# An encoder trunk on one core: another order of work in the mixer, and the wide products of gate and up ahead of the narrow ones

## The chip, the core and the metric

The kernel runs on one NeuronCore of a Trainium2 chip. The metric is the device time of one execution in microseconds (us), lower is better. Before the change the median of three runs is 956.33 us (955.96 to 956.51).

PE is the matrix engine (TensorE) and PEld its loads of stationary operands, DVE the vector engine, ACT the scalar engine, POOL GpSimd, SP the queue that issues the loads. PSUM has 8 banks, and each result of PE needs one until DVE or ACT has read it.

## What is computed

Two layers, each of three steps, on x of 256 tokens by 1024 columns, all in float32:

```python
def swiglu(x, w_in, w_out):
    h = x @ w_in
    gate, up = h[..., :D_FF], h[..., D_FF:]
    return (jax.nn.silu(gate) * up) @ w_out
...
    for l in range(DEPTH):
        x = layer_norm(ALPHA * x + 0.5 * swiglu(x, ffn1_w_in[l], ffn1_w_out[l]), ln_g[l, 0], ln_b[l, 0])
        mix = hybrid_mixer(x, cos, sin, mask, w_in[l], w_out[l], ...)
        x = layer_norm(ALPHA * x + mix, ln_g[l, 1], ln_b[l, 1])
        x = layer_norm(ALPHA * x + 0.5 * swiglu(x, ffn2_w_in[l], ffn2_w_out[l]), ln_g[l, 2], ln_b[l, 2])
```

D_FF is 2816. The mixer projects x once and splits the columns into two groups of heads. The first is differential attention: four heads with two score matrices each, softmax of both, the second subtracted with a learned weight, products with v, a root-mean-square norm. The second is attention in a window of 128 positions: eight query heads share two key and value heads, and a sink logit joins each softmax ("local" in the kernel's words). Queries and keys of both get rotary positions. Both outputs go side by side through one output projection.

## The kernel before, in words

**Split products.** Every float32 matrix is split into a high part in a reduced float format and a low remainder: ACT casts a weight tile (wh, line 80, 128x1024), DVE subtracts for the remainder (wl, line 81). A product is the sum of high by high, high by low and low by high. Weights come tile by tile through the class `Weights`: SP loads into 5 raw buffers, wh and wl have 9 buffers each, `get(i)` asks for tiles up to i+8. The casts have the lowest priority: the compiler's scheduler puts them into the queues of ACT and DVE wherever it sees nothing more urgent that is ready. Each queue is worked off in order. PE alone keeps the order of the program text.

**FFN.** `ffn` runs four times. `first` does the first four of 22 column tiles of gate and up for 128 tokens at a time. `col(j)` does each of the other 18, so 72 columns in all: for gate, then for up, 8 wide products (line 350: 512 moving columns, high weights by the high and low parts of x for both token tiles) and 8 narrow ones (line 352: 256 moving columns, low weights by the high part of x). Then ACT and DVE add the two halves, take silu, multiply and split again. `step` does the down projection (line 400), `layer_norm` follows for each token tile t.

**Mixer.** The order of PE's work is a text, `ORDER`, worked off token by token, the same for both layers:

- `P nm t c`: c of the four parts of the projection nm for token tile t (dq, dk, dv, sq: 6 products of 512 columns a part, lines 465 to 467; sk: 6 of 256). After the last part DVE turns the rotary positions (lines 481 to 491).
- `X`, `Z`: transposes of x for t=1 at the start and of the new x for t=0 at the end (line 273). Both need a finished layer norm.
- `T nm t`: transposes of queries or keys (line 501), after which ACT and DVE write the high and low parts (lines 503, 504).
- `S d t`, `S s t`: one unit of scores, 12 products of 64 rows (line 509) in two PSUM banks: two heads on the lower 64 partitions, two on the upper. Softmax follows on DVE and ACT (lines 522 to 535, or 551 to 572).
- `A t u`: 4 transposes of differential attention's weights (line 580), copied out by ACT (line 582). `V t`: its 16 products with v (line 594), then squares on ACT, a power on POOL, and y on DVE (lines 600 to 606).
- `W t n`: of local attention; n=0: 8 transposes (line 580), n=1: the other 8, and the 8 products of unit 0 with v (line 624), n=2: the 8 products of unit 1, after which the result is split (lines 634, 635).
- `Y t`: 4 transposes of y (line 273), split by lines 275 and 276. `O t c`: c of the 8 row tiles of the output projection (6 products each, line 688), and layer norm after the eighth. `G`: loads of the layer norm's constants.

In line 509 the three products of a score (high by high, high by low, low by high) stand together: three for the lower half of the partitions, then three for the upper, and so on.

Of the kernel before, what the change touches and what calls it, by code (L numbers as in the profile page):

```python
# [19 lines left out]
P = 128  # L20
SEQ = 256
D = 1024
KT = D // P
# [21 lines left out]


ORDER = """
P dq 0 3; P dk 0 2; P dq 0 1; P dk 0 1; X; P dk 0 1; P dq 1 1; P dv 1 1; P dv 0 1; P dk 1 1; P dv 0 1; P dv 1 1;
P dk 1 1; P dq 1 1; P dk 1 1; P dv 1 1; P dk 1 1; P dq 1 1; P dv 0 1; P dv 1 1; T dk 0; T dq 0; T dk 1; P sk 1
1; P sk 0 1; P dq 1 1; P dv 0 1; S d 0; S d 0; P sk 0 1; T dq 1; P sk 0 1; P sk 1 2; P sq 0 2; P sk 1 1; S d 1;  # L50
S d 1; P sk 0 1; P sq 0 2; A 0 1; A 0 0; T sk 1; P sq 1 2; T sq 0; T sk 0; V 0; A 1 0; S s 0; P sq 1 1; A 1 1; P
sq 1 1; G; V 1; S s 0; Y 0; T sq 1; O 0 3; S s 1; O 0 1; W 0 0; Y 1; S s 1; W 0 1; W 0 2; O 1 1; W 1 0; O 0 2; O
1 1; O 0 2; W 1 1; W 1 2; O 1 4; Z; O 1 2
"""
# [39 lines left out]
def encoder_kernel(  # L94
# [206 lines left out]
    def ffn(l, n, last=False):  # L301
# [39 lines left out]
        def col(j):  # L341
            nonlocal wi

            hs = [ps.tile([P, 2, SEQ], F32, tag="b", name=f"h{'gu'[s]}_{nm}_{j}") for s in range(2)]
            tl = tp.tile([P, 2, SEQ], F32, tag="tl", name=f"tl_{nm}_{j}", bufs=2)
            for s in range(2):
                wh, wl = W.get(wi)
                wi += 1
                for k in range(KT):
                    mm(hs[s], wh[:, k * P : (k + 1) * P], xx[:, k], start=(k == 0), stop=False)  # L350
                for k in range(KT):
                    mm(hs[s][:, 1, :], wl[:, k * P : (k + 1) * P], xx[:, k, 0], start=False, stop=(k == KT - 1))  # L352
                nc.scalar.copy(tl[:, s], hs[s][:, 1, :])  # L353
                dv.tensor_tensor(tl[:, s], hs[s][:, 0, :], tl[:, s], ALU.add)  # L354
# [77 lines left out]
    def mixer(l):  # L432
# [72 lines left out]

        def qk(o, q, k, a, h, kh, qt):
            b = slice(qt * P, (qt + 1) * P)
            for i, (m, n) in enumerate(((0, 0), (0, 1), (1, 0))):
                mm(o, q[m][a, h, b], k[n][a, kh, :], start=(i == 0), stop=(i == 2))


        def diff_scores(qt, u):
            nm = f"{l}{qt}{u}"
            with tc.high_priority():
                sc = [ps.tile([P, 2, SEQ], F32, tag="b", name=f"sd{nm}{c}") for c in range(2)]
                for i in range(2):
                    for c in range(2):
                        a = slice(64 * c, 64 * c + 64)
                        qk(sc[c][:, i, :], qT, kT, a, 2 * u + i, 2 * u + i, qt)
                mx = sp.tile([P, 4], F32, tag="mx", name=f"mxd{nm}")  # L520
# [17 lines left out]
        def swa_scores(qt, u):  # L538
            nm = f"{l}{qt}{u}"
            with tc.high_priority():  # L540
                sc = [ps.tile([P, 2, SEQ], F32, tag="b", name=f"ss{nm}{v}") for v in range(2)]
                for i in range(2):
                    for v in range(2):
                        a = slice(64 * v, 64 * v + 64)
                        qk(sc[v][:, i, :], sqT, skT, a, 2 * u + i, 0, qt)
                mx = sp.tile([P, 4], F32, tag="mx", name=f"mxs{nm}")
                sk = snk.rearrange("p (v u i) -> p u v i", v=2, u=2)[:, u]
                for v in range(2):
                    for i in range(2):
                        q = 2 * v + i  # L550
                        dv.tensor_tensor_reduce(sc[v][:, i, :], sc[v][:, i, :], mask[:, (1 - qt) * P : (3 - qt) * P], 1.0, sk[:, v, i : i + 1],
                                                ALU.add, ALU.max, mx[:, q : q + 1])
# [7 lines left out]
                den = sp.tile([P, 4], F32, tag="den", name=f"ds{nm}", bufs=8)  # L560
                for v in range(2):
                    for i in range(2):
                        q = 2 * v + i
# [4 lines left out]
                dv.reciprocal(rc, rc)  # L568
                for v in range(2):
                    for i in range(2):  # L570
                        q = 2 * v + i
# [36 lines left out]
        def swa_pv(qt, units):  # L608
# [16 lines left out]

            def part(n):
                with tc.high_priority():
                    if n < 2:
                        tr_(n)
                    if n > 0:  # L630
                        mm_(n - 1)
                    if n == 2:
                        dh = xx[:, 4:8, 0, qt, :]
# [40 lines left out]

        def do_w(q, n):
            if n == 0:
                sw[q] = swa_pv(q, units["s", q])
            sw[q](n)

# [16 lines left out]
        for tok in ORDER.split(";"):  # L696
# [15 lines left out]
            elif op == "V":  # L712
                ok = num("A", ar[0], 0) and num("A", ar[0], 1) and full("dv", 0) and full("dv", 1)
            elif op == "W":
                ok = (ar[1] < 2 or all(full(nm, ar[0]) for nm in heads)) and num("S", "s", ar[0]) > min(ar[1], 1) and (ar[1] == 0 or num("W", ar[0], ar[1] - 1))
            elif op == "Y":
                ok = all(full(nm, ar[0]) for nm in heads) and num("V", ar[0])
            elif op == "O":
                ok = num("Y", ar[0]) and num("G") and (rows(ar[0]) + ar[1] <= 4 or num("W", ar[0], 2))
            elif op == "Z":  # L720
                ok = rows(0) == KT
            else:
                ok = True
# [16 lines left out]
            elif op == "V":  # L740
                diff_pv(ar[0], units["d", ar[0]], pTs[ar[0]], y[ar[0]])
            elif op == "W":
                do_w(*ar)
            elif op == "Y":
# [83 lines left out]
```

## Time and profile before

| | |
|---|---|
| median of three runs | 956.33 us (955.96 to 956.51) |
| the profiled execution, its own time | 955.75 us |
| its span, first to last instruction | 954.0 us |
| PE busy | 942.0 us (99%) |
| DVE busy | 669.2 us (70%) |
| ACT busy | 510.4 us (54%) |
| granted clock of TensorE, mean | 0.998 of full speed |
| chain that ended last, PE's share | 90% |
| first mixer | from about 189.3 us to 290.5 us |
| second mixer | from about 660.3 us to 761.4 us |

A timeline row gives the start of a group of like instructions, its length up to the end of the last one, the engine, the line, the operation, the tiles, the form and the count; in brackets stands the idle time of the engine before it and what ended it. PE's instructions overlap: a wide product is shown as 0.39 us long, while the next one starts some 0.23 us after it. So the pace of PE is read from one start to the next, and not from lengths.

### The profile page before, as it was taken

The numbers are of one execution on the slowest core, as the hardware profiler recorded it, in microseconds if no ns is written. First come the engines' busy times: TensorE is split into PE (matmuls) and PEld (weight loads), VectorE is DVE, ScalarE is ACT, GpSimd is POOL, SyncE is SP. The second block draws the span as 40 slices with busy tenths as digits, with TensorE's granted clock in tenths as the row PEclk, the third lists the DMA queues.
The fourth block names the chain that finished last, engine by engine and source line by source line (L and its number), as shares of the span: only waits on it lengthen the run. The fifth ranks groups of instructions, "written<-read, shape, count | busy, mean of one in ns | idle before, by whom it ended". The sixth has DMA issues, their size and how long they took to land.

```text
span 954.0 us, 13703 instructions
## 1 busy us (share of the span) xinstructions
PE 942.0 (99%) x5087; PEld 801.7 (84%) x5087; DVE 669.2 (70%) x1103; ACT 510.4 (54%) x889; POOL 17.0 (2%) x27
## 2 busy tenths in 40 slices
PE   9999999999999999999999999999999999999997
PEld 6888888888778888888888888888887888888886
DVE  7887754688987776754687767447889877767434
ACT  5767543436765655553356565433477656565420
POOL 0000000000000000000000000000000000000000
PEclk9999999999999999999999999999999999999999
DMA  9886555366316755555376555553743366565521
GB/s 326 311 281 204 195 177 198 124 226 189 106 67 208 260 194 183 193 179 197 126 257 223 189 185 190 183 194 123 260 124 112 114 226 223 188 189 187 179 64 45
DMA packets 51234, 176.42 MB, mean 185 GB/s; under 512 B 6240, under 2 KB 8032, under 8 KB 51168
## 3 DMA queue, kind: packets, MB, share of 16 engines
q1 hardware_dynamic: 50896, 175.42, 56.0%
q8 instruction: 40, 0.66, 0.3%
q14 instruction: 26, 0.21, 0.1%
q10 hardware_dynamic: 272, 0.13, 0.0%
HBM read 174.48 MB, written 1.05 MB: 184 GB/s over the span
## 4 chain that ended last, share of the span: by engine, by line
PE 90%; DVE 6%; ACT 2%; issue 1%; POOL 0%; DVEq 0%
PE acc L400 25%; PE hg L350 14%; PE hu L350 14%; PE hb L318 9%; PE hu L352 7%; PE hg L352 7%; PE ao L688 4%; DVE wl L81 1%; ACT ed L528 1%; PE os L624 1%; PE pj_dq L467 1%; PE pj_dq L466 1%; PE pj_dk L467 1%; PE pj_dq L465 1%; PE pj_dk L466 1%
## 5 line engine op out<-in xcount | busy, mean ns | idle before, releaser
L81 DVE TENSOR_TENSOR wl<-raw,wh 128x1024 fp32r<-128x1024 f32 (+1 forms) x319 | 385.4, 1212 | 210.2 <-ACT wh L80 206.2
L80 ACT CAST wh<-raw 128x1024 fp32r<-128x1024 f32 (+1 forms) x319 | 332.5, 1046 | 323.8 <-PE acc L400 123.7
L400 PE MATMUL acc<-wh,g 128*128 128x512 f32 (+1 forms) x748 | 192.7, 377 | 0.0
L400 PEld LDWEIGHTS acc<-wh,g 128*128 128x128 f32 x748 | 136.0, 188 | 25.8
L350 PE MATMUL hg<-xx,wh 128*128 128x512 f32 x576 | 144.8, 393 | 0.0
L350 PE MATMUL hu<-xx,wh 128*128 128x512 f32 x576 | 144.2, 392 | 0.0
L350 PEld LDWEIGHTS hg<-xx,wh 128*128 128x128 f32 x576 | 103.6, 189 | 18.6
L350 PEld LDWEIGHTS hu<-xx,wh 128*128 128x128 f32 x576 | 103.6, 189 | 18.5
L400 PE MATMUL acc<-wl,g 128*128 128x512 f32 (+1 forms) x374 | 111.3, 377 | 0.0
L352 PEld LDWEIGHTS hg<-xx,wl 128*128 128x128 f32 x576 | 78.6, 190 | 5.7
L352 PEld LDWEIGHTS hu<-xx,wl 128*128 128x128 f32 x576 | 78.6, 190 | 5.6
L352 PE MATMUL hu<-xx,wl 128*128 128x256 f32 x576 | 80.3, 282 | 0.0
L352 PE MATMUL hg<-xx,wl 128*128 128x256 f32 x576 | 80.3, 282 | 0.0
L400 PEld LDWEIGHTS acc<-wl,g 128*128 128x128 f32 x374 | 68.9, 188 | 13.2
L318 PE MATMUL hb<-wh,xx 128*128 128x512 f32 x256 | 70.2, 391 | 0.0
L318 PEld LDWEIGHTS hb<-wh,xx 128*128 128x128 f32 x256 | 47.9, 188 | 10.5 <-ACT wh L80 0.7
L318 PE MATMUL hb<-wl,xx 128*128 128x512 f32 x128 | 39.5, 390 | 0.0
L688 PE MATMUL ao<-wh,xx 128*128 128x512 f32 x128 | 37.6, 400 | 1.1 <-ACT xx L275 1.1
L359 ACT CAST g<-tl 128x256 fp32r<-128x256 f32 x72 | 28.9, 402 | 8.1 <-DVE tl L357 8.0
L357 DVE TENSOR_TENSOR tl<-tl 128x256 f32<-128x256 f32 x72 | 30.5, 424 | 2.2
L354 DVE TENSOR_TENSOR tl<-hu,tl 128x256 f32<-128x256 f32 x72 | 30.0, 417 | 2.8 <-ACT tl L353 2.8
L360 DVE TENSOR_TENSOR g<-tl,g 128x256 fp32r<-128x256 f32 x72 | 30.1, 419 | 2.0 <-ACT g L359 1.9
(182 smaller groups left out, 940.7 us busy)
## 6 DMA issues: line engine op xcount, KB each, us to landing
raw<-in_f_in_dram SPq DMA_DIRECT2D x144, 512.0 KB, 4.1
raw<-in_f_out_dram SPq DMA_DIRECT2D x88, 512.0 KB, 3.4
raw<-in_m_in_dram SPq DMA_DIRECT2D x36, 512.0 KB, 3.5
raw<-in_f_b_dram SPq DMA_DIRECT2D x29, 512.0 KB, 3.4
raw<-in_m_out_dram SPq DMA_DIRECT2D x8, 512.0 KB, 4.5
raw<-in_m_out_dram SPq DMA_DIRECT2D x16, 256.0 KB, 4.2
lng<-in_ln_g_dram SPq DMA_DIRECT2D x6, 512.0 KB, 5.8
lnb<-in_ln_b_dram SPq DMA_DIRECT2D x6, 512.0 KB, 6.1
```

Of the source, the lines that this page charges most:

```text
L80: nc.scalar.copy(wh[:, s], raw[:, s])
L81: nc.vector.tensor_tensor(wl[:, s], raw[:, s], wh[:, s].bitcast(F32), ALU.subtract)
L318: mm(hb[s], xx[:, k, g, t, :], ww[:, 512 * s : 512 * s + 512], start=(k == 0 and e == 0), stop=(k == KT - 1 and e == 2))
L350: mm(hs[s], wh[:, k * P : (k + 1) * P], xx[:, k], start=(k == 0), stop=False)
L352: mm(hs[s][:, 1, :], wl[:, k * P : (k + 1) * P], xx[:, k, 0], start=False, stop=(k == KT - 1))
L354: dv.tensor_tensor(tl[:, s], hs[s][:, 0, :], tl[:, s], ALU.add)
L357: dv.tensor_tensor(gv, tl[:, 0], gv, ALU.mult)
L359: nc.scalar.copy(gs[q][:, jj, 0, :], gv)
L360: dv.tensor_tensor(gs[q][:, jj, 1, :], gv, gs[q][:, jj, 0, :].bitcast(F32), ALU.subtract)
L400: mm(a, g, ww[:, s], start=(k == 0 and e == 0), stop=(k == JT - 1 and e == 2))
L466: mm(o, xx[:, k, 0, t, :], wl[:, s], start=False, stop=False)
L688: mm(acc[t][h], xx[:, k, g, t, :], ww[:, s], start=(k == 0 and e == 0), stop=(k == KT - 1 and e == 2))
```

## The change

Three edits.

1. In `col` both weight tiles are asked for at once, and the order is: 8 wide products of gate, 8 wide of up, 8 narrow of gate, 8 narrow of up. Every product stays.
2. `qk` takes both halves of the partitions: each of the three products of a score is issued for the lower half and then for the upper. In local attention's softmax the loops over the head in the unit (i) and the half (v) change places.
3. The transposes of local attention are a token of their own, `B t n` (8 transposes, unit n), and `W t n` is its 8 products alone (n=0, 1). `ORDER` is a new text. The counts of all other tokens stay.

```diff
 ORDER = """
-P dq 0 3; P dk 0 2; P dq 0 1; P dk 0 1; X; P dk 0 1; P dq 1 1; P dv 1 1; P dv 0 1; P dk 1 1; P dv 0 1; P dv 1 1;
-P dk 1 1; P dq 1 1; P dk 1 1; P dv 1 1; P dk 1 1; P dq 1 1; P dv 0 1; P dv 1 1; T dk 0; T dq 0; T dk 1; P sk 1
-1; P sk 0 1; P dq 1 1; P dv 0 1; S d 0; S d 0; P sk 0 1; T dq 1; P sk 0 1; P sk 1 2; P sq 0 2; P sk 1 1; S d 1;
-S d 1; P sk 0 1; P sq 0 2; A 0 1; A 0 0; T sk 1; P sq 1 2; T sq 0; T sk 0; V 0; A 1 0; S s 0; P sq 1 1; A 1 1; P
-sq 1 1; G; V 1; S s 0; Y 0; T sq 1; O 0 3; S s 1; O 0 1; W 0 0; Y 1; S s 1; W 0 1; W 0 2; O 1 1; W 1 0; O 0 2; O
-1 1; O 0 2; W 1 1; W 1 2; O 1 4; Z; O 1 2
+P dk 0 1; P dq 0 3; P dk 0 1; X; P dk 0 2; P dq 1 1; P dk 1 1; P dq 0 1; P dv 0 1; P dv 1 1; P dq 1 1; P dv 1 1;
+P dq 1 1; P dk 1 3; P dv 0 1; P dv 1 1; P dq 1 1; P dv 1 1; T dk 0; T dq 0; T dk 1; P sk 1 1; P sk 0 1; P dv 0
+2; S d 0; S d 0; T dq 1; P sk 0 2; P sk 1 3; P sq 0 2; T sk 1; P sk 0 1; S d 1; A 0 0; P sq 0 1; A 0 1; S d 1; T
+sk 0; P sq 0 1; P sq 1 2; G; T sq 0; V 0; S s 0; A 1 0; P sq 1 1; A 1 1; P sq 1 1; Y 0; V 1; S s 0; O 0 1; T sq
+1; O 0 3; S s 1; B 0 0; B 0 1; Y 1; W 0 0; W 0 1; S s 1; O 1 1; O 0 1; O 1 1; O 0 3; B 1 0; B 1 1; O 1 1; W 1 0;
+W 1 1; O 1 1; Z; O 1 4
 """
...
+            ws = [W.get(wi), W.get(wi + 1)]
+            wi += 2
             for s in range(2):
-                wh, wl = W.get(wi)
-                wi += 1
                 for k in range(KT):
-                    mm(hs[s], wh[:, k * P : (k + 1) * P], xx[:, k], start=(k == 0), stop=False)
+                    mm(hs[s], ws[s][0][:, k * P : (k + 1) * P], xx[:, k], start=(k == 0), stop=False)
+            for s in range(2):
                 for k in range(KT):
-                    mm(hs[s][:, 1, :], wl[:, k * P : (k + 1) * P], xx[:, k, 0], start=False, stop=(k == KT - 1))
+                    mm(hs[s][:, 1, :], ws[s][1][:, k * P : (k + 1) * P], xx[:, k, 0], start=False, stop=(k == KT - 1))
...
-        def qk(o, q, k, a, h, kh, qt):
+        def qk(os, q, k, h, kh, qt):
             b = slice(qt * P, (qt + 1) * P)
             for i, (m, n) in enumerate(((0, 0), (0, 1), (1, 0))):
-                mm(o, q[m][a, h, b], k[n][a, kh, :], start=(i == 0), stop=(i == 2))
+                for c, o in enumerate(os):
+                    a = slice(64 * c, 64 * c + 64)
+                    mm(o, q[m][a, h, b], k[n][a, kh, :], start=(i == 0), stop=(i == 2))
...
-            def part(n):
+            def part(op, n):
                 with tc.high_priority():
-                    if n < 2:
+                    if op == "B":
                         tr_(n)
-                    if n > 0:
-                        mm_(n - 1)
-                    if n == 2:
+                    else:
+                        mm_(n)
+                    if op == "W" and n == 1:
                         dh = xx[:, 4:8, 0, qt, :]
                         nc.scalar.copy(dh, o)
```

## Rows read from the trace of the kernel before

**Rows 1.** The page, its first part: busy time, share of the span, instructions.

```profile
PE 942.0 (99%) x5087; PEld 801.7 (84%) x5087; DVE 669.2 (70%) x1103; ACT 510.4 (54%) x889; POOL 17.0 (2%) x27
```

**Rows 2.** The chain that ended last, FFN stretches: start, length, instructions.

```profile
27.30 1.81 PE hg L350 x8
...
36.53 1.84 PE hu L350 x8
39.32 1.84 PE hg L350 x8
...
128.71 57.83 PE acc L400 x255
```

**Rows 3.** Timeline of PE, wide products behind 18 narrow ones, first mixer.

```profile
230.76 0.40 PE L465 MATMUL pj_sq<-wh,xx 128*128 128x512 f32 x1
...
232.14 0.39 PE L465 MATMUL pj_sq<-wh,xx 128*128 128x512 f32 x1
```

**Rows 4.** Timeline of PE, scores of differential attention, first mixer.

```profile
225.72 1.69 PE L509 MATMUL sd<-dkT,dqT 64*128 64x256 f32 x24
227.35 0.39 PE L465 MATMUL pj_sk<-wh,xx 128*128 128x256 f32 x1
...
234.31 1.80 PE L509 MATMUL sd<-dkT,dqT 64*128 64x256 f32 x24
236.04 0.39 PE L465 MATMUL pj_sk<-wh,xx 128*128 128x256 f32 x1
```

**Rows 5.** Timeline of PE around T sq 0 and the first S s 0.

```profile
239.61 1.03 PE L580 MATMUL tpd<-ident,ed 128*128 128x128 f32 x8
...
243.13 0.39 PE L467 MATMUL pj_sq<-wh,xx 128*128 128x512 f32 x1
243.74 0.63 PE L501 MATMUL tq_sq<-ident,r_sq 128*128 128x128 f32 x4 [0.22 <-DVE wt L533]
...
244.32 1.95 PE L594 MATMUL od<-vd,pTd 128*128 128x128 f32 x16
...
246.63 0.38 PE L509 MATMUL ss<-skT,sqT 64*128 64x256 f32 x1
247.84 0.98 PE L509 MATMUL ss<-skT,sqT 64*128 64x256 f32 x11 [0.83 <-DVE skT L504]
```

**Rows 6.** Timeline of PE, later in the first mixer: transposes, and an S s 1.

```profile
254.87 0.66 PE L273 MATMUL tr_y<-ident,y 128*128 128x128 f32 x4
...
256.71 0.72 PE L688 MATMUL ao<-wh,xx 128*128 128x512 f32 x2 [0.52 <-ACT xx L275]
...
261.04 0.98 PE L509 MATMUL ss<-skT,sqT 64*128 64x256 f32 x12
...
265.77 0.66 PE L580 MATMUL tps<-ident,esw 128*128 128x128 f32 x4
266.74 0.66 PE L580 MATMUL tps<-ident,esw 128*128 128x128 f32 x4 [0.30 <-DVE xx L276]
...
278.42 1.03 PE L580 MATMUL tps<-ident,esw 128*128 128x128 f32 x8
```

**Rows 7.** Timeline of DVE, 242 to 253 us.

```profile
242.92 0.68 DVE L489 TENSOR_TENSOR r_sq<-m_sq,m_sq 128x512 f32<-128x512 f32 x1
...
244.64 2.35 DVE L81 TENSOR_TENSOR wl<-raw,wh 128x1024 fp32r<-128x1024 f32 x2
...
251.82 0.60 DVE L606 SCALAR_TENSOR_TENSOR y<-od,f,gsb 128x128 f32<-128x128 f32 x2
```

**Rows 8.** Timeline of ACT: the last exponential of the first S s 1.

```profile
267.93 0.54 ACT L564 ACTIVATE esw<-ss,mxs 128x256 f32<-128x256 f32 x1
```

**Rows 9.** Timelines of DVE and PE: ends of two layer norms, and X.

```profile
195.03 1.41 DVE L296 SCALAR_TENSOR_TENSOR x<-x,rs,lnb 128x512 f32<-128x512 f32 x2
...
198.83 1.03 PE L273 MATMUL tr_m<-ident,x 128*128 128x128 f32 x8
...
283.13 1.41 DVE L296 SCALAR_TENSOR_TENSOR x<-x,rs,lnb 128x512 f32<-128x512 f32 x2
```

More of the change, by code (lines that the diff above doesn't have):

```diff
@@ L516, in diff_scores @@
                 for i in range(2):
-                    for c in range(2):
-                        a = slice(64 * c, 64 * c + 64)
-                        qk(sc[c][:, i, :], qT, kT, a, 2 * u + i, 2 * u + i, qt)
+                    qk([s[:, i, :] for s in sc], qT, kT, 2 * u + i, 2 * u + i, qt)
                 mx = sp.tile([P, 4], F32, tag="mx", name=f"mxd{nm}")
@@ L542, in swa_scores @@
                 for i in range(2):
-                    for v in range(2):
-                        a = slice(64 * v, 64 * v + 64)
-                        qk(sc[v][:, i, :], sqT, skT, a, 2 * u + i, 0, qt)
+                    qk([s[:, i, :] for s in sc], sqT, skT, 2 * u + i, 0, qt)
                 mx = sp.tile([P, 4], F32, tag="mx", name=f"mxs{nm}")
                 sk = snk.rearrange("p (v u i) -> p u v i", v=2, u=2)[:, u]
-                for v in range(2):
-                    for i in range(2):
+                for i in range(2):
+                    for v in range(2):
                         q = 2 * v + i
@@ L560, in swa_scores @@
                 den = sp.tile([P, 4], F32, tag="den", name=f"ds{nm}", bufs=8)
-                for v in range(2):
-                    for i in range(2):
+                for i in range(2):
+                    for v in range(2):
                         q = 2 * v + i
@@ L568, in swa_scores @@
                 dv.reciprocal(rc, rc)
-                for v in range(2):
-                    for i in range(2):
+                for i in range(2):
+                    for v in range(2):
                         q = 2 * v + i
@@ L673, in do_a, with do_w @@
                 pTs.setdefault(q, {})[u] = (trans_p(e[:, 0, 0, :], e[:, 0, 1, :], f"d{l}{q}{u}"))
-        def do_w(q, n):
-            if n == 0:
+        def do_w(op, q, n):
+            if q not in sw:
                 sw[q] = swa_pv(q, units["s", q])
-            sw[q](n)
+            sw[q](op, n)
         def do_o(t, c):
@@ L713, in mixer @@
                 ok = num("A", ar[0], 0) and num("A", ar[0], 1) and full("dv", 0) and full("dv", 1)
+            elif op == "B":
+                ok = num("S", "s", ar[0]) > ar[1]
             elif op == "W":
-                ok = (ar[1] < 2 or all(full(nm, ar[0]) for nm in heads)) and num("S", "s", ar[0]) > min(ar[1], 1) and (ar[1] == 0 or num("W", ar[0], ar[1] - 1))
+                ok = num("B", ar[0], ar[1]) and (ar[1] == 0 or num("W", ar[0], 0) and all(full(nm, ar[0]) for nm in heads)) and full("sk", 0) and full("sk", 1)
             elif op == "Y":
@@ L718, in mixer @@
             elif op == "O":
-                ok = num("Y", ar[0]) and num("G") and (rows(ar[0]) + ar[1] <= 4 or num("W", ar[0], 2))
+                ok = num("Y", ar[0]) and num("G") and (rows(ar[0]) + ar[1] <= 4 or num("W", ar[0], 1))
             elif op == "Z":
@@ L741, in mixer @@
                 diff_pv(ar[0], units["d", ar[0]], pTs[ar[0]], y[ar[0]])
-            elif op == "W":
-                do_w(*ar)
+            elif op in ("B", "W"):
+                do_w(op, *ar)
             elif op == "Y":
```

## The prediction

> **What bounds the kernel now.** I read the busy times first: PE is busy for 99% of the span [rows 1]. So time can come only from two places: the pace at which PE starts products, and the few stretches in which it waits. Next I read the chain that ended last, for the pace in the FFN, and then PE's timeline through the mixer, start to start. Lengths are no help, since PE's rows overlap.
>
> In the chain 255 wide products of the down projection take 57.83 us, 0.2268 us each [rows 2]. Eight wide products of a column take 1.81 us where wide products stand ahead of them (the first column), but 1.84 us where narrow ones do. From one half of a column to the next it is 39.32 - 36.53 = 2.79 us, so the narrow eight take 0.95 us, 0.12 each [rows 2].
>
> In the mixer four stretches are longer than their work. Each occurs in both mixers, within 0.15 us of the same size; I price the first.
> (a) From the last sq product at 243.13 to T sq 0 at 243.74 it is 0.61 instead of 0.23: **0.38** lost [rows 5].
> (b) S s 0 starts at 246.63, stops after one product and ends at 247.84 + 0.98 = 248.82, 2.19 us; a unit that doesn't wait takes 0.98: **1.2** lost [rows 5, 6].
> (c) Eight transposes and their hand-over run from 254.87 to 256.71, 1.84 us, while five that don't wait take 244.32 - 243.74 = 0.58, so eight some 0.93: **0.9** lost [rows 5, 6].
> (d) Eight transposes from 265.77 end at 266.74 + 0.66 = 267.40, 1.63 us against the 1.03 of the same eight at 278.42: **0.6** lost [rows 6]. The row names DVE's L276: the second four want a PSUM bank that Y's transposes still hold.
> The sum is 3.1 us a mixer, 6.2 us in all. This is the most that a new order alone can bring back.
>
> **The change, part by part.**
>
> *Gate and up.* A column changes from narrow to wide once instead of twice. The eight wide products behind a change cost 1.84, eight at the steady pace 8 x 0.2268 = 1.814: 0.026 saved. The second eight narrow ones follow narrow ones and cost 8 x 0.12 = 0.96 instead of 0.95: 0.008 lost. That is 0.018 x 72 columns = **1.3 us saved**. It could be nothing, if the loss grew with the length of the narrow run; it could be 1.9 (0.026 x 72). For the middle speaks that behind 18 narrow products six wide ones take 1.38 us against 6 x 0.2268 = 1.36, no more than behind eight [rows 3]. Gate's low weights are held 1.9 us longer and up's high ones are wanted 0.9 us earlier. PE's waits show no weight, and ACT's casts wait for PE to free buffers, so this costs nothing; that cover would have to shrink by more than a column's 5.6 us to show. Gate's result comes 0.9 us later, and what uses it is the down projection, many columns on.
>
> *Score products.* The text of the kernel has three for one half, then three for the other. The trace shows 24 products from 225.72 to 227.35, 1.63 us [rows 4]. One after the other at the narrow pace they would need 24 x 0.12 = 2.9; twelve pairs need 1.44, and 0.19 goes for entering. So PE already runs the halves side by side. The second group needs 236.04 - 234.31 = 1.73, so alternating has 0.1 to win there, once a mixer. Against it: the two S d 1 are now apart, with A 0 0, P sq 0 1 and A 0 1 between them, which makes one more visit to the half-array form, some 0.3 (0.19 from rows 4 and as much again as a half at its borders). But W 0 1 now hands straight to S s 1, and several S stand beside transposes instead of wide products, which returns some 0.2. Sum: **0** a mixer, bounds -0.3 to +0.4.
>
> The Trainium skill says otherwise of the old order ("TensorE: Matmul & The Clock Gate", Part 3, "The mechanism"): matmuls start and end strictly in program order. By that rule only the borders between threes could overlap. The trace disagrees: 1.63 us is below what that rule allows. What it would give is a rival below.
>
> *Waits that go.* (c) goes: V 1 and an S s 0, some 2.7 us of work, stand between Y 0 and the first O. (d) goes in its old place: the B's come ahead of Y 1. (a) and (b) change cover:
> - (a) From the last sq product for t=0 (239.61) to the end of r_sq it took 242.92 + 0.68 - 239.61 = 3.99 us [rows 5, 7]. Of that PE now covers only P sq 1 2, 12 x 0.2268 plus a slow start, 2.85 us, since both A's and T sk 1 moved ahead. So 0 (if DVE does its three steps of 0.68 at once) to 1.15; I take 0.6, in the middle, since S d 1's second unit now ends closer to it and keeps DVE busy.
> - (b) From T sq 0 to the score product that waits it took 247.84 - 243.74 = 4.10 us [rows 5], of which 2.35 on DVE are two weight casts that got in first [rows 7]. Cover up to the first score product is now T sq 0 and V 0, 0.47 + 1.79 = 2.3, instead of 2.9, and DVE has 0.3 less to do, since T sk 0 came earlier. So 0 to 1.5; I take 0.7, because the wait in (a) gives the casts time to be done ahead of it.
> - Y 0 needs y. From the end of V 0 (244.32 + 1.95 = 246.27) to the last y (251.82 + 0.60 = 252.42) it took 6.15 us [rows 5, 7]. Now S s 0 with its wait, two A and two P cover 1.1 + 0.7 + 0.9 + 2.8 = 5.5. So 0 to 0.7; I take 0.3.
> - Banks. At S s 1, B 0 0, B 0 1 the two of the output, two of scores and four of transposes are all eight. Y 1, W 0 and the output of t=1 then wait for ACT to copy or to finish its exponentials. A unit of S s 1 held its banks from 261.04 to 267.93 + 0.54 = 268.47, 7.4 us [rows 6, 8]; the output of t=1 now wants one after some 6.0 (0.9 + 1.75 + 0.45 + 1.9 + 0.95). So 0 to 1.4; I take 0.4, since most of ACT's delay there came from the stretch (d) itself.
> - X comes two parts (2.72 us) earlier, at 196.11. The layer norm ends at 195.03 + 1.41 = 196.44, and its first half 0.66 before [rows 9]; the second half is wanted at 196.55. Z has 5.9 us of work between itself and the eighth O 0; layer norm took from 278.42 to 284.54, 6.1 us [rows 6, 9], its first half 5.5, and the second half is wanted 0.44 later than Z's start. Both just fit: 0 to 1.1 together, if a cast of 1.2 slips in; I take 0.2.
>
> *Loads.* G's two loads of the layer norm's constants are issued ahead of T sq 0 instead of behind the last sq product. The first product now asks for dk's tile, and so for four tiles more; the loads keep the order of their numbers on SP. The waits of PE and ACT name loads of FFN weights alone, none of the mixer's, so both cost nothing; if a buffer came free late, it would show as a product that waits for line 80 or 81.
>
> New waits: 0.6 + 0.7 + 0.3 + 0.4 + 0.2 = 2.2 a mixer against 3.1 before: 0.9 saved, **1.8 us** in both.
>
> **Sum.** -1.3 - 1.8 = -3.1 us. The profiled execution's own time, 955.75, becomes 952.65; it lies 0.58 below the median of the runs shown, so the forecast against the median 956.33 is **953.2 us**. 0.2%, about what a measurement of this kernel can tell from no change, is 1.9 us.
>
> **The rivals.**
> 1. *The waits only move.* If each chain keeps its old length, (a) costs 1.15, (b) 1.5, y 0.5, the rest 0.1: 3.25, a little over the old sum. Left is the FFN's 1.3, less 0.3: 955.3. For it: the same engines, and casts that fill the same gaps. Against it: (c) and (d) were waits at a hand-over that now has 2 us and more of work in it.
> 2. *The new covers hold.* Waits of 0.5 a mixer: 2 x 2.6 + 1.3 = 6.5 saved, 949.8. For it: without the casts (b)'s chain fits its cover, and everything else fits by its short bound. Against it: three covers fit with 0.1 us to spare.
> 3. *PSUM's eight banks become the bound: slower.* Place: B 0 0 to O 1 1. If ACT does four exponentials (4 x 0.54) ahead of the copies of the B's, Y 1 and W 0 wait 2.2, and the output of t=1 another 1.4: 3.6 instead of 0.4 a mixer, 6.4 more: 959.6. It decides from a wait of 2.9 a mixer there (0.4 and half of 958.2 - 953.2). For it: the sum of exactly eight, and the changed loops free both score banks late. Against it: the copies can start 0.6 us after each four transposes, while the exponentials have to wait for DVE first.
> 4. *Order in PE is strict after all*: a product never passes one ahead of it. Then threes overlap at borders only: 7 of 24 and 3 of 12 instead of 12 and 6, and alternating saves 5 and 3 slots of 0.12 in 4 and 8 groups, 44 x 0.12 = 5.3 us more: 947.9. Against it stands the 1.63 us [rows 4]: 17 slots would be 2.04 us. (This is the rule of the Trainium skill named above.)
>
> **How the numbers follow.** Forecast 0.42 (its own range 952.0 to 954.4), rival 1 0.25, rival 2 0.20, rival 3 0.10, rival 4 0.03. Faster by over 0.2% means below 954.4: the forecast but for 0.02, and rivals 2 and 4: 0.63. Within 0.2%: rival 1 and that 0.02: 0.27. Slower: rival 3, 0.10. The range leaves out rival 3 and the lower half of rivals 2 and 4: 949.8 to 956.6, the top being rival 1 without the FFN's gain.
>
> **What would show it.** In the new profile the columns start every 5.57 us instead of 5.59, with 16 wide products in 3.65. Every group of scores shows 24 products in 1.63 or 12 in 0.92, as now. (c)'s stretch is gone. T sq 0 and the first S s 0 still wait on DVE, 1.3 together. Wrong I would be if the columns keep 5.59 (the slow start then follows the number of narrow products), if S s groups get shorter than 0.9 (rival 4), or if the waits of PE name ACT's line 564 or 582 for more than 2.9 us a mixer (rival 3).

## The result, and the profile after

The changed kernel takes **949.42 us** (median, 948.71 to 949.65) against 956.12 us for the kernel before on the same chip: ratio 0.9929, 95% interval 0.9919 to 0.9939. It is faster, as forecast, but by 6.7 us where 3.1 were forecast, and 949.42 lies 0.4 us below the range.

The page of the changed kernel: busy time, and the shares of the chain that ended last.

```profile
PE 938.9 (99%) x5087; PEld 800.6 (84%) x5087; DVE 663.0 (70%) x1103; ACT 529.7 (56%) x889; POOL 17.0 (2%) x27
...
PE 96%; DVE 2%; DMA 1%; SPq 0%; issue 0%; ACT 0%; DVEq 0%
```

PE's instructions are as many as before and its busy time is 3.1 us less [rows 1]; its share of the chain rose from 90% to 96%. The span fell from 954.0 to 947.7, by 6.3 (the profiled execution of before lies 0.4 us below its median), and starts on PE's timeline say where. The mixers take 98.57 and 98.56 us instead of 101.18 and 101.12 (from the first projection's start, 189.18 in the first, to the next FFN's first product, 287.75): 5.2 less. The two FFNs between the mixers take 369.17 instead of 369.84, the last one 192.20 instead of 192.53: 1.0 less. The rest is at the start. The chain that ended last, in the FFN of the changed kernel (start, length, instructions):

```profile
33.91 1.84 PE hg L351 x8
35.76 1.81 PE hu L351 x8
...
39.48 1.84 PE hg L351 x8
...
128.55 57.83 PE acc L402 x255
```

A column lasts 39.48 - 33.91 = 5.57 us, sixteen wide products 3.65, and only the first eight show the slow 1.84. The down projection keeps its 57.83 [rows 2]. All waits of PE in the changed kernel (line, releaser: us in total, times, longest; the first is the start of the program):

```profile
PE wps L164 <- DVE wz L161: 1.2, 1, 1.2
PE ss L514 <- DVE sqT L506: 0.5, 2, 0.2
```

Of the four waits of before one is left. PE's timeline, first mixer, in the places that answer to [rows 4 to 6]:

```profile
225.60 1.69 PE L514 MATMUL sd<-dkT,dqT 64*128 64x256 f32 x24
227.22 0.66 PE L503 MATMUL tq_dq<-ident,r_dq 128*128 128x128 f32 x4
...
240.89 0.40 PE L467 MATMUL pj_sq<-wh,xx 128*128 128x512 f32 x1
...
243.40 0.39 PE L469 MATMUL pj_sq<-wh,xx 128*128 128x512 f32 x1
243.63 0.60 PE L503 MATMUL tq_sq<-ident,r_sq 128*128 128x128 f32 x4
...
245.95 0.50 PE L514 MATMUL ss<-skT,sqT 64*128 64x256 f32 x4
246.68 0.74 PE L514 MATMUL ss<-skT,sqT 64*128 64x256 f32 x8 [0.23 <-DVE sqT L506]
247.34 0.66 PE L581 MATMUL tpd<-ident,ed 128*128 128x128 f32 x4
...
251.06 0.60 PE L274 MATMUL tr_y<-ident,y 128*128 128x128 f32 x4
...
260.42 0.97 PE L514 MATMUL ss<-skT,sqT 64*128 64x256 f32 x12
261.32 1.97 PE L581 MATMUL tps<-ident,esw 128*128 128x128 f32 x16
263.12 0.60 PE L274 MATMUL tr_y<-ident,y 128*128 128x128 f32 x4
```

The 24 products take 227.22 - 225.60 = 1.62. T sq 0 comes 0.23 us behind the last sq product: wait (a) is gone. S s 0 takes 247.34 - 245.95 = 1.39 where a unit that doesn't wait takes 261.32 - 260.42 = 0.90: 0.49 is left of (b). Transposes of y, their hand-over and all 16 local transposes (1.80) run without a stop: (c), (d) and PSUM's banks cost nothing. DVE's timeline in the same stretch:

```profile
238.34 1.21 DVE L82 TENSOR_TENSOR wl<-raw,wh 128x1024 fp32r<-128x1024 f32 x1
...
241.09 0.69 DVE L483 TENSOR_TENSOR m_sq<-pj_sq,cos_t 128x512 f32<-128x512 f32 x1
...
242.48 0.69 DVE L491 TENSOR_TENSOR r_sq<-m_sq,m_sq 128x512 f32<-128x512 f32 x1
...
244.80 1.22 DVE L82 TENSOR_TENSOR wl<-raw,wh 128x1024 fp32r<-128x1024 f32 x1
245.94 0.68 DVE L506 TENSOR_TENSOR sqT<-tq_sq,sqT 128x512 fp32r<-128x512 f32 x1
...
261.18 0.17 DVE L569 RECIPROCAL rs<-rs 128x4 f32<-128x4 f32 x1
...
261.39 1.14 DVE L573 TENSOR_SCALAR esw<-esw,rs 128x256 f32<-128x256 f32 x4
262.44 0.49 DVE L552 CUSTOM_DVE_ANT_0 ss<-ss,mask,snk 128x256 f32<-128x256 f32 x1
```

Three things to see. The rotary steps run almost back to back, from 241.09, and r_sq is there at 243.17, ahead of T sq 0: 2.28 us behind t=0's last sq product (240.89), where the prediction's (a) read 3.99 in the kernel before. One weight split (L82, 1.2 us) stands ahead of the queries' remainder (sqT), where two did before [rows 7]; another is done at 238.34 already. And the four multiplications of the local softmax (L573) stand together, ahead of the next unit's masks (L552).

### The profile page after: what moved, and what is told of

Same layout as the page of the kernel before. It is cut to its first block, busy times and chain, and to the rows that moved or that the text cites. A ratio compares the mean times of both kernels' runs of the same rounds, so it can differ in the third digit from the quotient of the medians.

```text
span 947.7 us, 13757 instructions
## 1 busy us (share of the span) xinstructions
PE 938.9 (99%) x5087; PEld 800.6 (84%) x5087; DVE 663.0 (70%) x1103; ACT 529.7 (56%) x889; POOL 17.0 (2%) x27
## 4 chain that ended last, share of the span: by engine, by line
PE 96%; DVE 2%; DMA 1%; SPq 0%; issue 0%; ACT 0%; DVEq 0%
PE acc L402 25%; PE hg L351 14%; PE hu L351 14%; PE hb L319 8%; PE hu L354 7%; PE hg L354 7%; PE ao L689 5%; PE os L625 1%; PE pj_dk L467 1%; PE pj_dk L469 1%; PE tps L581 1%; PE pj_dv L467 1%; PE pj_dv L468 1%; PE pj_dv L469 1%; PE pj_dk L468 1%; PE pj_dq L468 1%
## 5 line engine op out<-in xcount | busy, mean ns | idle before, releaser
L82 DVE TENSOR_TENSOR wl<-raw,wh 128x1024 fp32r<-128x1024 f32 (+1 forms) x319 | 385.5, 1210 | 169.2 <-ACT wh L81 100.8
L351 PE MATMUL hu<-xx,wh 128*128 128x512 f32 x576 | 142.3, 389 | 0.0
L351 PEld LDWEIGHTS hu<-xx,wh 128*128 128x128 f32 x576 | 108.1, 188 | 22.6
L354 PEld LDWEIGHTS hu<-xx,wl 128*128 128x128 f32 x576 | 74.3, 192 | 0.0
L355 ACT COPY tl<-hu 128x256 f32<-128x256 f32 x72 | 26.8, 373 | 35.1 <-PE hu L354 35.1
L357 ACT ACTIVATE tl<-tl 128x256 f32<-128x256 f32 x72 | 30.3, 420 | 17.8 <-DVE tl L356 17.8
```

The lines of the kernel that those rows point to most:

```text
L82: nc.vector.tensor_tensor(wl[:, s], raw[:, s], wh[:, s].bitcast(F32), ALU.subtract)
L351: mm(hs[s], ws[s][0][:, k * P : (k + 1) * P], xx[:, k], start=(k == 0), stop=False)
L354: mm(hs[s][:, 1, :], ws[s][1][:, k * P : (k + 1) * P], xx[:, k, 0], start=False, stop=(k == KT - 1))
L357: nc.scalar.activation(tl[:, 0], tl[:, 0], AF.Silu)
```

## The experiments

All 17 kernels at once. "Mixers" are their two lengths in us, read as above; the kernel before measured 955.75 to 956.14 us beside them. The second column is a median, while the ratio follows the means: three of a10_ahead's ten runs lie 1.4 to 3.4 us above its median, so its ratio is higher than its median says.

| kernel | us | ratio to before, 95% interval | mixers |
|---|---|---|---|
| ffn_only | 954.57 | 0.9984 [0.9975, 0.9993] | 101.13, 101.09 |
| alternate_only | 957.94 | 1.0021 [1.0012, 1.003] | 102.19, 102.12 |
| order_only | 950.98 | 0.9948 [0.9936, 0.9961] | 98.78, 98.73 |
| halves_apart | 956.15 | 1.0 [0.9991, 1.0009] | 101.22, 101.26 |
| y0_ahead | 957.93 | 1.0019 [1.0009, 1.0028] | 102.21, 101.82 |
| local_block | 959.61 | 1.0035 [1.0022, 1.0049] | 102.80, 102.82 |
| sd1_together | 949.98 | 0.9935 [0.9919, 0.9952] | 98.91, 98.93 |
| a10_ahead | 954.27 | 0.9988 [0.9979, 0.9998] | 100.88, 100.86 |
| a10_raised | 950.27 | 0.9941 [0.9926, 0.9956] | 99.00, 99.00 |
| masks_between | 954.08 | 0.9982 [0.9973, 0.9991] | 100.71, 101.11 |
| alt_raised | 955.97 | 1.0001 [0.9992, 1.0011] | not read |
| local_raised | 956.65 | 1.0009 [0.9999, 1.0018] | 101.48, 101.41 |
| y0_raised | 956.27 | 1.0002 [0.9992, 1.0011] | 101.25, 101.27 |
| halves_raised | 956.28 | 1.0002 [0.9993, 1.0011] | 102.13, 102.18 |
| column_pairs | 948.17 | 0.9917 [0.9904, 0.9931] | 98.48, 98.51 |
| early_half | 955.87 | 1.0001 [0.9991, 1.001] | 101.68, 101.72 |
| late_half | 951.61 | 0.9956 [0.9942, 0.9971] | 99.67, 99.68 |

### The change in its parts

**ffn_only**: the kernel before with edit 1 (the new `col`) alone.

> The kernel before with edit 1 alone: 16 wide products of gate and up, then 16 narrow ones. Theory A (a slow start belongs to each change from narrow to wide): 0.0195 us a column, 72 columns, 1.4 us faster, ratio 0.9985, the columns every 5.567 us; the mixers stay at 101.1 us. Rival (the FFN's part in the changed kernel came from the mixer's order, for instance from casts that moved): no change, columns still every 5.587 us.

It gives 1.5 us, and its mixers are those of before.

**alternate_only**: the kernel before with the alternating products of edit 2 alone; the softmax loops stay.

```diff
-                mm(o, q[m][a, h, b], k[n][a, kh, :], start=(i == 0), stop=(i == 2))
+                for c, o in enumerate(os):
+                    a = slice(64 * c, 64 * c + 64)
+                    mm(o, q[m][a, h, b], k[n][a, kh, :], start=(i == 0), stop=(i == 2))
```

> The kernel before with the products of a score issued alternately for the two halves, and nothing else. Theory A (PE lets a product of the other half pass those that wait ahead of it, so the threes were side by side already): 0.1 us a mixer, 0.2 in all, ratio 0.9998; the second group of 24 takes 1.63 us instead of 1.73, the others stay at 1.63 and 0.91. Rival (products start strictly in order): 44 slots of 0.12 us, 5.3 us faster, ratio 0.9945, groups of 12 in 0.7 us or less.

This missed: PE's own work got shorter (the second group of 24 products from 234.92 to 236.54, 1.62 instead of 1.73 [rows 4]), and the kernel got 1.8 us slower. Two of PE's waits in alternate_only are new in this size, both at the local transposes:

```profile
PE tps L579 <- DVE esw L571: 1.5, 1, 1.5
...
PE tps L579 <- DVE mxs L556: 1.1, 1, 1.1
```

**order_only**: the changed kernel without edit 1 and without the alternation (new `ORDER`, B and W apart, softmax loops exchanged).

> The changed kernel without edit 1 and without the alternation: the new order, B and W apart, and the exchanged loops of the softmax. Theory A (the order carries nearly all of the mixers' gain, since its waits fell from 3.1 to about 0.6 us a mixer): 5.0 us faster, ratio 0.9948, mixers of 98.6 to 98.8 us. Rival (the order alone brings what I forecast, and the alternation or its effect on the waits the rest): 1.8 us faster, ratio 0.998, mixers of about 100.2 us.

It gives 5.1 us. With edit 1's 1.5 that is the whole 6.7, so the times leave nothing for alternating, which cost 1.8 in the old order. The traces have the mixers 0.2 shorter with it (98.78 to 98.57), and most of that is waits: in order_only T sq 0 still loses 0.16 (243.33 to 243.72, less 0.23) and S s 0 0.62 (246.06 to 247.59, less 0.91), in the changed kernel 0 and 0.49, and 0.15 at its first S d 1, where twelve products take 1.055 us instead of 0.91.

### Score products: how far does PE pass?

**halves_apart**: the kernel before, each unit's six products of the lower half ahead of the six of the upper.

```diff
-                for i in range(2):
-                    for c in range(2):
+                for c in range(2):
+                    for i in range(2):
```

> The kernel before with the scores' program order pushed apart: in each unit six products for the lower half, then six for the upper. Theory A (a product of the other half passes those that wait ahead of it, whatever their number here): groups of 12 and 24 keep about their length, at most 0.3 us more each where the first six run alone; within 0 to +2.5 us in all. Rival (strict order, or a passing distance of only three): 11 slots of 0.12 us for 12 products instead of 6, 0.6 us more a unit, 16 units, about 9 us slower.

The time stays, the groups don't. PE's timeline of halves_apart:

```profile
225.82 2.03 PE L509 MATMUL sd<-dkT,dqT 64*128 64x256 f32 x24
227.78 0.39 PE L465 MATMUL pj_sk<-wh,xx 128*128 128x256 f32 x1
```

24 products take 1.96 us instead of 1.63. In strict order a pair could form only at the three borders of six, 21 slots of 0.12 and 0.19 for entering, 2.7 us. So PE passes products here too, but not six far, if its queue holds them in the order of the text (the trace does not name a product's half). The lost 0.34 a group comes back in shorter waits, which is why the time doesn't show it: PE had time to lose there.

### Single steps moved

**sd1_together**: the changed kernel, S d 1's units together again.

```diff
-S d 1; A 0 0; P sq 0 1; A 0 1; S d 1; T sk 0;
+A 0 0; P sq 0 1; A 0 1; S d 1; S d 1; T sk 0;
```

> The changed kernel with the two units of S d 1 together again (P sq 0 1; A 0 1; S d 1; S d 1; T sk 0), where the change put the split of sk 0 between them. Theory (the wait at T sq 0 is gone because S d 1 was taken apart and work put between): a wait of 0.4 to 1.2 us a mixer comes back at T sq 0 or at the second unit, ratio to before 0.9938 to 0.9955, mixers 99.0 to 99.8 us. Rival (it is gone because of what stands ahead of T sq 0 in VectorE's queue): mixers stay at 98.6 us, ratio 0.993.

The wait at T sq 0 comes back with 0.60 (243.92 - 243.09 - 0.23), and the mixers get 0.35 longer, a little under the theory's span. PE's timeline of sd1_together:

```profile
243.09 0.39 PE L464 MATMUL pj_sq<-wh,xx 128*128 128x512 f32 x1
243.92 0.63 PE L498 MATMUL tq_sq<-ident,r_sq 128*128 128x128 f32 x4 [0.44 <-DVE rd L529]
```

**y0_ahead**: the kernel before, one step moved.

```diff
-G; V 1; S s 0; Y 0; T sq 1;
+G; Y 0; V 1; S s 0; T sq 1;
```

> The kernel before with one step moved: Y 0 stands ahead of V 1 and S s 0 instead of behind them. Before, the products of ao waited 0.9 us a mixer for the transposed y of t=0. Theory (a wait of TensorE is a step that stands too near behind its producer): the wait at ao goes, -0.4 to -0.9 us a mixer, so ratio 0.998 to 0.999 and mixers of 100.2 to 100.8 us. Rival (the end of y 0 sets the time whatever TensorE does meanwhile): the wait moves to Y 0's transposes, mixers stay at 101.1 us, ratio 1.000.

Neither came: wait (c) is gone, PE's ao no longer waits, and yet the mixers are 0.7 to 1.0 us longer. A wait of 1.4 us at the local transposes, for DVE's L567 (esw), has taken its place, and T sq 1 waits 0.5 us for DVE's L484 (r_sq).

**local_block**: the kernel before, the local steps as in the change.

```diff
-O 0 1; W 0 0; Y 1; S s 1; W 0 1; W 0 2; O 1 1; W 1 0; O 0 2; O 1 1; O 0 2; W 1 1; W 1 2; O 1 4
+O 0 1; B 0 0; B 0 1; Y 1; W 0 0; W 0 1; S s 1; O 1 1; B 1 0; O 0 2; O 1 1; O 0 2; B 1 1; W 1 0; W 1 1; O 1 4
```

> The kernel before with the local block's steps alone as the change has them (transposes B of three heads, Y 1, then products W of three heads, for both t), the old order elsewhere, no alternation, the old softmax loops and the old FFN. Theory: the wait for the PSUM bank at the local transposes (0.6 us a mixer) goes, mixers 100.4 to 100.6 us, ratio 0.9988. Rival (two kinds of user of the two banks follow one another without a gap): the transposes wait for the scores' banks, mixers at or above 101.1 us, ratio 1.000 or more.

1.7 us a mixer longer, and not for a bank: behind the split and the masks the first multiplication of the second unit comes at 264.47 (261.39 in the changed kernel), and the ninth transpose starts at 264.97. A second wait of 0.8 us for a multiplication stands at the transposes of t=1.

**a10_ahead**: the changed kernel, A 1 0 moved to cover the 0.49 us that S s 0 still waits.

```diff
-V 0; S s 0; A 1 0;
+V 0; A 1 0; S s 0;
```

> The changed kernel with the step A 1 0 (some 0.44 us of TensorE's work) moved ahead of S s 0, whose first unit waits 0.49 us a mixer. Theory (the producer's end is fixed and any work put ahead covers the wait): 0.44 us a mixer is saved, ratio to before 0.9920, mixers 98.1 us. Rival (VectorE's and ScalarE's queues get another order with the moved step, and the producer ends later by as much): mixers at 98.5 us or more, ratio 0.993 or above.

S s 0's wait falls to 0.07 us, as meant, and the kernel loses 4.9 us. PE's timeline of a10_ahead at the local transposes:

```profile
265.42 0.44 PE L576 MATMUL tps<-ident,esw 128*128 128x128 f32 x2 [1.22 <-DVE esw L568]
```

DVE's timeline of a10_ahead ahead of that:

```profile
261.41 0.17 DVE L564 RECIPROCAL rs<-rs 128x4 f32<-128x4 f32 x1
261.50 1.20 DVE L77 TENSOR_TENSOR wl<-raw,wh 128x1024 fp32r<-128x1024 f32 x1
262.61 0.87 DVE L568 TENSOR_SCALAR esw<-esw,rs 128x256 f32<-128x256 f32 x3
263.40 0.49 DVE L547 CUSTOM_DVE_ANT_0 ss<-ss,mask,snk 128x256 f32<-128x256 f32 x1
...
265.01 0.35 DVE L568 TENSOR_SCALAR esw<-esw,rs 128x256 f32<-128x256 f32 x1
```

Here is what all four losses have in common. Behind the same reciprocal, where the changed kernel has its four multiplications at once, DVE does a weight split, three multiplications, the four masks of the next unit and then the fourth, which PE needs: it ends at 265.36 instead of 262.53. The text of DVE's work is the same in both; the scheduler put it into another order, because one step of PE had moved. alternate_only, y0_ahead and local_block also have a split and the four masks ahead of a multiplication that PE waits for; whether this is the cause is tried below.

The kernel before has the same split (261.93) and masks in this place, but Y 1 and a unit of S s 1 stand ahead of its second unit's transposes, so that PE wants these multiplications from 265.77 on and loses less. DVE's timeline of the kernel before:

```profile
263.04 0.49 DVE L551 CUSTOM_DVE_ANT_0 ss<-ss,mask,snk 128x256 f32<-128x256 f32 x1
...
265.33 0.62 DVE L572 TENSOR_SCALAR esw<-esw,rs 128x256 f32<-128x256 f32 x2
...
265.99 0.69 DVE L276 TENSOR_TENSOR xx<-tr_y,xx 128x512 fp32r<-128x512 f32 x1
```

L276 is the step that wait (d) named. It reads ACT's cast of the same transposes (L275), which ended at 265.65; the other 0.34 us it stood behind the late multiplications.

### VectorE's queue, with PE's order untouched

The next kernels change only the priority with which the scheduler places the last six steps of the local softmax:

```diff
-                rc = sp.tile([P, 4], F32, tag="rc", name=f"rs{nm}", bufs=8)
-                dv.tensor_tensor(rc, den, es, ALU.add)
+                with tc.high_priority(40):
+                    rc = sp.tile([P, 4], F32, tag="rc", name=f"rs{nm}", bufs=8)
+                    dv.tensor_tensor(rc, den, es, ALU.add)
...
```

**a10_raised**: a10_ahead with that.

> The kernel a10_ahead (the changed kernel with A 1 0 ahead of S s 0), TensorE's order untouched; only the last steps of the local softmax (sum, reciprocal, four multiplications) get a higher priority with the scheduler, so that they stand in VectorE's queue ahead of the masks of the next unit, and the weight split of 1.2 us no longer stands among them. Theory (the 2.3 us a mixer that a10_ahead lost are the place of that split and of the masks in VectorE's queue): mixers 98.1 to 98.7 us instead of 100.9, ratio to before 0.992 to 0.9935. Rival (the loss is in TensorE's own order or in the PSUM banks): mixers stay at or above 100.3 us, ratio 0.9975 or more.

Against the kernel before beside each, 3.8 of the 4.9 us come back. The mixers miss the theory's upper end by 0.3. One part of what is left is Y 0: its four transposes take 0.99 us instead of 0.43. a10_ahead has the same 0.99 (250.95 to 251.94), so this came with the moved step, and the priority neither made nor mended it.

**masks_between**: the changed kernel with the priority 10, which puts the next unit's masks between the second and the third multiplication.

> The changed kernel with TensorE's order untouched; only the priority of the same six steps of the local softmax is set so that in VectorE's queue the four masks of the next unit (0.41 us each, 1.6 in all) stand between the second and the third multiplication of a unit. Theory (VectorE's queue decides): the transposes of these weights wait 1.0 to 1.6 us a mixer at one place or at two, mixers 99.6 to 101.5 us, ratio to before 0.995 to 0.999. Rival (the order of TensorE's text decides, and the queue has room for it): mixers at 98.6 us, ratio 0.993.

As the theory says: the two mixers are 4.7 us longer than the changed kernel's, with the same text for PE. All waits of PE in masks_between for DVE's multiplications:

```profile
PE tps L582 <- DVE esw L574: 3.1, 2, 1.6
```

DVE's timeline of masks_between:

```profile
261.72 0.62 DVE L574 TENSOR_SCALAR esw<-esw,rs 128x256 f32<-128x256 f32 x2
262.25 0.49 DVE L552 CUSTOM_DVE_ANT_0 ss<-ss,mask,snk 128x256 f32<-128x256 f32 x1
...
263.87 0.35 DVE L574 TENSOR_SCALAR esw<-esw,rs 128x256 f32<-128x256 f32 x1
```

DVE does the masks first although the third multiplication's inputs were there with the second's. The Trainium skill has it so ("TensorE: Matmul & The Clock Gate", Part 1, "Architectural detail: the array is 16× 32×32, not 1× 128×128"): VectorE's queue is strictly first in, first out. The trace agrees, 1.6 us at a time.

**alt_raised** and **local_raised**: alternate_only and local_block with the priority 40.

> The kernel alternate_only (before with alternating score products alone, 2.0 us slower than before) with the same six steps of the local softmax raised in priority and nothing else. Theory (its loss was the weight split and the masks ahead of the last multiplications in VectorE's queue, a wait of 1.5 us at the local transposes): mixers 100.4 to 101.2 us instead of 102.2, ratio 0.998 to 1.000. Rival (alternating itself costs it): mixers stay at 102.2 us, ratio 1.002.

> The kernel local_block (before with the local block's steps as in the change, 3.5 us slower than before) with the same six steps of the local softmax raised in priority and nothing else. Theory (its waits of 2.2 us a mixer at the local transposes come from VectorE's queue): mixers 100.4 to 101.0 us instead of 102.8, ratio 0.998 to 0.9995. Rival (the transposes standing together want more PSUM banks than there are): the waits stay at 1.5 us or more a mixer, mixers 102.0 us or more, ratio 1.002 or more.

alt_raised gets all of its loss back (957.94 to 955.97; only its time is read, so that the wait itself went is not seen). local_raised gets 2.8 of 3.5 us back against the kernel before beside each, 1.35 a mixer, less than expected; its local transposes no longer wait for a bank or a split, but 0.5 us remains for esw at another place.

**y0_raised**: y0_ahead with the priority 40.

> The kernel y0_ahead (before with Y 0 moved ahead of V 1, 1.8 us slower than before) with the last six steps of the local softmax raised in priority and nothing else. Theory (the wait for y was worth 0.4 to 0.9 us a mixer, and VectorE's queue hid it): mixers 100.2 to 100.8 us, ratio to before 0.998 to 0.9995. Rival (moving Y 0 gains nothing, whatever the queue): mixers at 101.1 us or more, ratio 1.000 or more.

The rival's time: the wait at the local transposes is gone, and T sq 1 now waits 0.64. Almost all of y0_ahead's loss comes back, but nothing is gained for the 0.9 us that (c) cost. PE's timeline of y0_raised:

```profile
254.73 0.99 PE L504 MATMUL ss<-skT,sqT 64*128 64x256 f32 x12
256.35 0.66 PE L496 MATMUL tq_sq<-ident,r_sq 128*128 128x128 f32 x4 [0.64 <-DVE r_sq L484]
```

**halves_raised**: the changed kernel, mixer tiles split in two halves on DVE, priority 20.

```diff
-                nc.vector.tensor_tensor(wl[:, s], raw[:, s], wh[:, s].bitcast(F32), ALU.subtract)
+                for d in range(c, c + n, n // (2 if 66 <= i % 158 < 104 else 1)):
+                    h = slice(d, d + n // (2 if 66 <= i % 158 < 104 else 1))
+                    nc.vector.tensor_tensor(wl[:, h], raw[:, h], wh[:, h].bitcast(F32), ALU.subtract)
```

> The changed kernel with the weight splits of the mixer's tiles done on VectorE in two halves of some 0.6 us instead of one of 1.2, and the last six steps of the local softmax raised in priority by 20; TensorE's order untouched. Theory (a wait left over is one whole split that stands ahead of an urgent step): the 0.49 us at S s 0 falls to 0.1 or less, mixers 97.9 to 98.3 us, ratio to before 0.9915 to 0.9925. Rival (the queue is worked off in another order and a new wait appears): mixers at 98.6 us or more.

S s 0's wait goes (0.90 us for the unit), but new ones come: 1.5 at the transposes of t=1, 0.7 at T sq 0, 0.6 at a projection that now waits for a split. It is a new queue, and a worse one; which of the two edits, the halves or the priority, made it so was not tried.

How full that queue is shows in a window of 237 to 267 us: PE, PEld, DVE, ACT and POOL busy, of 30.00 us. First the kernel before:

```profile
237.00:267.00 30.00, 28.10 (x189) 22.91 (x188) 28.41 (x94) 22.80 (x76) 2.03 (x2) 1.00 0.32 108
```

The changed kernel:

```profile
237.00:267.00 30.00, 29.77 (x214) 24.45 (x213) 28.00 (x90) 24.38 (x78) 2.03 (x2) 1.00 0.33 108
```

DVE is busy for 95% and 93% of it. PE's idle time went from 1.9 to 0.2 us with DVE about as full.

### Do covers add up?

**early_half**, **late_half**: the changed kernel with the new order up to V 0 and the old one behind it, and the other way round.

> The changed kernel with the new order up to V 0 alone; from there the old order (A 1 0 ahead of S s 0, V 1 and S s 0 ahead of Y 0, Y 1 and a unit of S s 1 between the local transposes). In its queue on VectorE a weight split and the four masks of the next unit stand among the local softmax's multiplications, as in alternate_only. Theory (the queue decides): the waits at T sq 0 and S s 0, 1.6 us a mixer before, shrink to 0.6 or less, and 1.0 to 2.0 come back at the local transposes: mixers 100.6 to 102.0 us, ratio to before 0.998 to 1.001. Rival (covers add up one by one): the early waits go, the late ones stay as before: mixers 99.9 to 100.2 us, ratio 0.996.

> The changed kernel with the old order up to V 0 and the new one from there. In its queue on VectorE no split and no mask stands among the first eight local multiplications, as in the changed kernel. Theory (the queue decides): almost all but the early waits of before is gained: the waits at T sq 0 and S s 0 stay at 1.0 to 1.6 us a mixer, nothing else waits, mixers 99.2 to 99.9 us, ratio 0.9945 to 0.996, so that the two halves together gain less than the whole (2.6 us a mixer). Rival (covers add up one by one): the halves' gains add up to 2.4 to 2.8 us a mixer.

Both mixers' lengths fall where the theory has them. early_half lengthens a mixer by 0.5 to 0.6 us, late_half shortens it by 1.5; together 1.0, the whole 2.6. In early_half T sq 0 and S s 0 lose next to nothing. The local transposes wait, and (c), with Y 0 in its old place, takes 2.28 us (253.71 to 255.99) instead of the 0.93 that its work needs. PE's timeline of early_half:

```profile
264.67 0.88 PE L576 MATMUL tps<-ident,esw 128*128 128x128 f32 x6 [1.58 <-DVE esw L568]
```

late_half keeps the early waits; start to start they are 2.0 us, some more than expected. PE's timeline of late_half:

```profile
243.90 0.63 PE L498 MATMUL tq_sq<-ident,r_sq 128*128 128x128 f32 x4 [0.34 <-DVE wt L531]
...
248.00 0.74 PE L509 MATMUL ss<-skT,sqT 64*128 64x256 f32 x8 [1.26 <-DVE skT L501]
```

### Edit 1, taken further

**column_pairs**: the changed kernel, two columns at a time.

```diff
-        def col(j):
+        def col(*js):
...
+            for j in js:
+                for s in range(2):
+                    for k in range(KT):
+                        mm(hs[j][s], ws[j][s][0][:, k * P : (k + 1) * P], xx[:, k], start=(k == 0), stop=False)
+            for j in js:
...
```

> The changed kernel with two columns of gate and up at a time: 32 wide products, then 32 narrow ones, for 16 of the 17 columns behind the first in each FFN. This takes away 8 of 18 changes from narrow to wide in each FFN. Theory (0.018 us for each change): 0.6 us less in the four FFNs, the FFNs between the mixers 368.9 us instead of 369.17, the last one 192.05, ratio to before 0.9923. Rival (weights held longer or a longer narrow run cost it): the FFNs between the mixers at 369.2 us or more, and waits of TensorE or of ScalarE's casts for weights in the trace.

In the direction that the theory says, and 948.17 us is the fastest of all kernels here. The chain that ended last, in column_pairs:

```profile
44.54 1.84 PE hg L354 x8
46.38 1.81 PE hu L354 x8
48.19 1.81 PE hg L354 x8
50.01 1.81 PE hu L354 x8
...
55.65 1.84 PE hg L354 x8
```

One eight of four is slow, and a pair lasts 11.11 us against 2 x 5.567 = 11.134: 0.02 for each change from narrow to wide that goes, 0.6 to 0.8 for the 32 that go in all. The FFNs between the mixers take 368.76 us (369.07 to 369.17 in the other kernels with edit 1). The intervals overlap (0.9904 to 0.9931, the changed kernel's 0.9919 to 0.9939), so the gain rests on these rows; that the medians differ by more, 1.25 us, is not shown to be the columns.

## Why the prediction was right or wrong

- **Gate and up: right.** Forecast 1.3, measured 1.5 alone; the column's 5.57 us and the sixteen wide products' 3.65 came as written, and column_pairs confirms the reason.
- **Score products: right in the new order.** Forecast 0, bounds -0.3 to +0.4 a mixer; by the traces 0.2 saved, most of it waits, as order_only shows. Strict order in PE is refuted once more: groups stay at 0.90 and 1.62 us. What the step did not see is alternate_only: the same edit in the old order costs 1.8 us, which the priority on DVE's steps gives back.
- **Waits that go: right that they go, half wrong on why.** (c) went by Y 0's new place: it is gone in y0_ahead and back in early_half. For (d) the prediction named a bank held by Y's transposes. DVE's step that frees it came late in part (0.34 us) because of the multiplications ahead of it; the new local block by itself made its own place worse by 1.7 us a mixer, and the priority alone took 1.35 of it away.
- **New waits: the step that failed.** "New waits: 0.6 + 0.7 + 0.3 + 0.4 + 0.2 = 2.2 a mixer". Measured: (a) 0, (b) 0.49, y 0, banks 0, X and Z 0, and 0.15 that was not listed, at the first S d 1: 0.64. The 1.56 too much is 3.1 us in both mixers, of the 3.4 by which these beat the forecast (5.2 saved instead of 1.8). The bounds held each value. The fault was to take near the middle of five ranges as if they were five independent prices, each from the old length of a chain against PE's new cover. The chains did not keep that length: (a)'s is 2.28 us instead of 3.99, and (b)'s, from T sq 0 to the product that waits, 246.68 - 243.63 = 3.05 instead of 4.10. Their length hangs on the order of DVE's queue, which the scheduler makes anew for every order of PE, and which is full in this stretch. The changed kernel's queue gives nearly all the low ends together; others cost 1.2 to 1.6 us of waiting a mixer, as in a10_ahead, early_half, local_block and masks_between. That all five prices hang on this one queue is not shown: the runs move it at the local transposes, and the early waits only together with PE's order.
- **The rivals.** Rival 2 (949.8) named the outcome and part of the reason, "without the casts (b)'s chain fits its cover": one cast went ahead of T sq 0, the other stayed, and so did 0.49 us. Rival 3 did not come: sixteen transposes in 1.80 us. A rival on the slower side that was real was missing: the weight split and the masks ahead of the local multiplications, 1.2 to 1.6 us at a time (0.65 to 0.8 at each of two places in local_block).
- **The range** left out the lower half of rival 2, and the result fell there.
- **Open**: why the scheduler finds the good order for this text. That splits stand early in it (238.34 in the changed kernel) is seen; which buffer or cast lets them was not tried.

## What to carry to other kernels

Where a second engine's queue is as full as here (93 to 95% busy), do not take a wait of the first engine for a hole that work will cover: in a10_ahead, y0_ahead and local_block moved steps changed that queue, and a wait came out elsewhere. Before pricing a new order, read what stands ahead of each releaser in its own queue, and move the waits' prices together, all low or one high. If a scheduler makes the queue, give the steps that the first engine waits for a priority, and look at the queue again after every move.

## What the runs showed of the hardware that was not expected

PE runs products of the two halves of the partitions side by side even where three of one half stand ahead of three of the other, and with six ahead of six it still does so in part: 24 products in 1.62 us alternating, 1.63 to 1.73 by threes, 1.96 by sixes. In the first group of halves_apart two products start alone, then nearly all in pairs 5 to 10 ns apart, and three alone at the end; if a pair is one product of each half, the first upper one passed three lower ones. All this holds if PE's queue keeps the order of the text, as the kernel's description says. The Trainium skill ("TensorE: Matmul & The Clock Gate", Part 3, "The mechanism") has matmuls start and end in program order; by that rule the sixes would need 2.7 us, as worked out above from rows. The trace disagrees, with 1.96. Other orders were not tried.
